# A two-layer streaming encoder on one core: the modulation's first pieces land in spare slots, and three projections of layer 0 run as float32r passes

## The chip, the core and the metric

The kernel runs on one core of a Trainium2 chip. What counts is the device time of one execution in microseconds (us). The kernel before took 2290.78 us, the median of three runs (2288.68 to 2294.38). One more execution was taken with the profiler on; it took 2285.5 us, and all durations below come from it.

## The reference, cut to what matters

x has 256 positions of 2048 channels, c is one row of 2048. Each of two layers computes six modulation rows from c, then an input projection of the normalised and modulated x, whose columns feed four groups of mixers, an output projection, and a gated feed-forward block. The part that matters here is the start of layer 0:

```
c_act = silu(c)
mod = (c_act @ w_mod[l] + b_mod[l]).reshape(bn, 6, d)      # 2048 x 12288
shift_m, scale_m, gate_m = mod[:, 0], mod[:, 1], mod[:, 2]
h = layer_norm(x) * (1.0 + scale_m) + shift_m
proj = h @ w_in[l]                                         # 2048 x 4288
uv, q_c, kv_c, k_r, sb, sc, sh, ag = split(proj)
y_a = gmlp(uv)          # U (512 columns) and V (512)
y_b = attention(q_c, kv_c, k_r)                            # B
y_c = sb * conv3(sc * sh)                                  # E (sb) and C (sc, sh)
y_d = silu(layer_norm(conv31(a * sigmoid(g))))             # D: a, g = split(ag), 1024 columns
```

## The kernel before, in words

All engines work from lists of instructions in a fixed order: a scheduling layer records the program, gives each operation its place on its engine, and adds the waits. TensorE multiplies; VectorE, ScalarE and GpSimd work element by element; SyncE (SP) issues nearly all loads, in order. A load that has to wait for a buffer holds up all loads behind it. Loads take one of eight semaphores in turn, so a load also waits until the one eight places before it has landed.

A product in full float32 ("exact") has one instruction in the program and two matmul records in the trace. The other way is float32r: a float32 weight is cast to float32r (`whi`, ScalarE, L455), the rest is what VectorE subtracts (`wlo`, L456), the activations are split likewise (`hT`, L474 and L475), and three float32r products (hi by hi, hi by lo, lo by hi) take the place of the exact one. `weights` (L420) does one or the other: it loads into a buffer of the `raw` kind (4 of 1 MB) and splits into `whi` and `wlo` tiles (4 of each, 0.5 MB), or, for exact products, loads straight into `whi` and `wlo` tiles without a split.

The modulation runs on VectorE: each step (`mod_step`, L230 to L236) multiplies a loaded tile of w_mod by one value of c_act per partition and adds it to an accumulator (`qacc` or `macc`). TensorE then sums the accumulator's partitions with a column of ones (`ps_mod`), and VectorE adds the bias (L190, L192).

Layer 0 can't wait for the whole modulation. `by_pieces` (L1174) therefore cuts the 2048 channels into pieces of k tiles of 128: two tiles, two, four, four and four (here pieces 0 to 4). `mod_piece` (L238) makes shift and scale of one piece: 16 row tiles of w_mod, four steps to a raw buffer in the small pieces (512 wide) and two in the others (1024 wide), so that the small pieces take 16 steps of 512 and the others 16 of 1024. `finish` in `piece` (L1378) takes the sums, modulates the normalised x (`hF`, half on ScalarE, half on VectorE) and splits it into `hT`.

For each piece TensorE adds the k tiles' share to four projections: D (1024 columns), which keeps four of the six PSUM accumulators through all pieces, and U, V and E (512 each), which use the other two in turn. `side` (L1202) computes their share and adds it to sums in SBUF: ScalarE copies PSUM out (`part`, L1220), VectorE adds (L1221); in the last piece VectorE adds from PSUM (L1217). D's products run in float32r from the fifth k tile on (pieces 2 to 4); U, V and E stay exact in all pieces. The work of a piece is woven in four turns: a quarter of D, then U, V or E after each of the first three; the steps for the next piece's modulation are put between them by shares (`some_mods`), and the next piece's `finish` stands ahead of the fourth quarter of D.

After the last piece: `mix_d` (GLU: two sigmoids on ScalarE, two products on VectorE, then a list of 124 conv taps and the norm as background work), `mix_u`, `gelu_v` and `mix_v` (the gMLP), then the exact projections B (768 columns) and C (1024), during which the background list is worked off at seven and eight entries a unit, and a stream of further modulation rows (w_mod, 1 MB a step) is fed at a rate for each phase (RATES). Then comes the output projection (`out_proj`), whose first 1024 columns are float32r.

Slots are 11 tiles of 0.5 MB for activations. Four of them hold `hF` from the start of layer 0 to the end of C; the other seven stand empty while the pieces run.

Of the kernel before, what the change touches and what calls it, by code (L numbers as in the profile page):

```python
# [13 lines left out]
P = 128  # L14
D = 2048
# [3 lines left out]
KT = D // P  # L19
# [25 lines left out]
PIECES = ((0, 2), (2, 2), (4, 4), (8, 4), (12, 4))  # L45

PLAIN_KT = 4


@with_exitstack  # L50
def encoder_kernel(ctx: ExitStack, tc: tile.TileContext, A: dict, consts: bass.AP, out: bass.AP):
# [14 lines left out]
    def raw_tile(name):  # L66
        return rawp.tile([P, 2048], F32, tag="raw", name=name)
# [7 lines left out]
    def acc_tile(name):  # L75
        return accp.tile([P, 512], F32, tag="acc", name=name)

    def mm(o, lhsT, rhs, start, stop):
        pe.matmul(o, lhsT, rhs, start=start, stop=stop, skip_group_check=True)  # L79
# [4 lines left out]
    def slot(name, dtype=F32):  # L84
        return slotp.tile([P, 1024], dtype, tag="slot", name=name)
# [113 lines left out]
    def sum_cols(l, m, k0, acc):  # L199

        n = acc.shape[1] // P
        ps = ms_tile("ps_mod")
        for j in range(n):
            mm(ps[:, j : j + 1], acc[:, j * P : (j + 1) * P], ones[:, 0:1], True, True)
        mod_cols(l, m, k0, ps, n)
# [24 lines left out]
    def mod_step(acc, w, kt, first):  # L230
        col = cact[:, kt : kt + 1]
        if first:
            i = dve.tensor_scalar(out=acc, in0=w, scalar1=col, scalar2=None, op0=ALU.mult)
        else:
            i = dve.scalar_tensor_tensor(out=acc, in0=w, scalar=col, in1=acc, op0=ALU.mult, op1=ALU.add)  # L235
        held(i, "mod")  # L236

    def mod_piece(l, ms, k0, nkt):  # L238


        n, width = len(ms), nkt * P
        nk = 2048 // (n * width)
        acc = tmpp.tile([P, D], F32, tag="macc", name="qacc", bufs=2)[:, : n * width]
        units = []

        def unit(u):
            raw = raw_tile("wmod").rearrange("p (k m c) -> p k m c", k=nk, m=n)
            for i, m in enumerate(ms):
                c0 = m * D + k0 * P
                nc.sync.dma_start(  # L250
                    out=raw[:, :, i, :],
                    in_=A["w_mod"][l, u * nk * P : (u + 1) * nk * P, c0 : c0 + width].rearrange(
                        "(k p) c -> p k c", p=P
                    ),
                )
            for k in range(nk):
                mod_step(acc, raw[:, k, :, :].rearrange("p m c -> p (m c)"), u * nk + k, u == 0 and k == 0)

        for u in range(KT // nk):
            units.append(lambda u=u: unit(u))  # L260

        def sums():
            for i, m in enumerate(ms):
                sum_cols(l, m, k0, acc[:, i * width : (i + 1) * width])

        return units, sums
# [122 lines left out]
    background = []  # L389
# [21 lines left out]
    def held(i, kind):  # L411

        name, n = hold[kind]
        if n > 0:
            hold[kind][1] = n - 1
            tc.add_manual_dep(i.ins, name, order_dep, reason="the norm is what the next products wait for")
# [45 lines left out]
    def act_pair(name):  # L462

        both = actp.tile([P, 4 * S], F32R, tag="act", name=name).rearrange("p (k h t) -> p k h t", k=2, h=2)
        return [both[:, :, 0, :], both[:, :, 1, :], both]
# [708 lines left out]
    def by_pieces(l, w_in, hF, between, mix_d, mix_u, gelu_v, mix_v, mix_b, mix_c, mix_e):  # L1174


        hf = lambda kt: hF[kt // 4][:, kt % 4, :]
        accD = [acc_tile(f"D{l}_c{i}") for i in range(4)]
        sums = {}
        for g in "UVE":  # L1180
            both = actp.tile([P, 1024], F32, tag="act", name=f"sum{g}")
            sums[g] = [both[:, i * 512 : (i + 1) * 512] for i in range(2)]
        cols = {"U": C_UV, "V": C_UV + 512, "E": C_SB}

        hT[:] = [None] * (PLAIN_KT // 2) + [act_pair("hT") for _ in range((KT - PLAIN_KT) // 2)]

        def terms(kt, part):

            hi, lo = part
            if lo is None:  # L1190
                return [(hi, hf(kt))]
            xh, xl = (h[:, kt % 2, :] for h in hT[kt // 2][:2])
            return [(hi, xh), (hi, xl), (lo, xh)]

        def chan_major(ps, kt, part, blocks, first, last):
            ts = terms(kt, part)
            for i in blocks:
                o = ps[i // 2][:, (i % 2) * S : (i % 2 + 1) * S]
                for n, (w, x) in enumerate(ts):
                    mm(o, w[:, i * P : (i + 1) * P], x, first and n == 0 and i % 2 == 0, last and n == len(ts) - 1)  # L1200

        def side(g, parts, k0, nkt):  # L1202
            ps = [acc_tile(f"{g}{l}_{i}") for i in range(2)]
            for kt, part in parts:
                st, sp = kt == k0, kt == k0 + nkt - 1
                if g == "V":
                    ts = terms(kt, part)
                    for t in range(2):
                        for n, (w, x) in enumerate(ts):
                            mm(ps[t], x[:, t * P : (t + 1) * P], w, st and n == 0, sp and n == len(ts) - 1)  # L1210
                else:
                    chan_major(ps, kt, part, range(4), st, sp)
            for i in range(2):
                if k0 == 0:
                    act.copy(sums[g][i], ps[i])
                elif k0 + nkt == KT:
                    dve.tensor_tensor(out=sums[g][i], in0=ps[i], in1=sums[g][i], op=ALU.add)  # L1217
                else:
                    part = tmp_tile("part")
                    act.copy(part, ps[i])  # L1220
                    dve.tensor_tensor(out=sums[g][i], in0=part, in1=sums[g][i], op=ALU.add)  # L1221

        first = between(0)[1]
        first()
        for q, (k0, nkt) in enumerate(PIECES):
            ahead = between(q + 1) if q + 1 < len(PIECES) else ([], None)
            exact = k0 < PLAIN_KT
            loaded = {}

            def load(g, kt):  # L1230

                c0, width = (C_AG, 1024) if g == "D" else (cols[g], 512)
                nk = min(2048 // width, nkt)
                for j, p in enumerate(weights(w_in, kt, nk, c0, width, exact or g != "D")):
                    loaded[(g, kt + j)] = p

            mods_left = list(ahead[0])
            units = len(mods_left)

            def some_mods(share):  # L1240
                while mods_left and (units - len(mods_left)) < units * share:
                    mods_left.pop(0)()

            def d_part(kt, half):
                if ("D", kt) not in loaded:
                    load("D", kt)
                chan_major(accD, kt, loaded[("D", kt)], range(4 * half, 4 * half + 4), kt == 0, kt == KT - 1)

            turns_d = [(kt, h) for kt in range(k0, k0 + nkt) for h in range(2)]
            n = len(turns_d) // 4  # L1250
            for s in range(4):
                mine = turns_d[s * n : (s + 1) * n]
                if ("D", mine[0][0]) not in loaded:
                    load("D", mine[0][0])
                some_mods((0.3, 0.7, 1.0, 1.0)[s])
                if s == 3 and ahead[1] is not None:
                    ahead[1]()
                for kt, h in mine:
                    d_part(kt, h)
                if s < 3:  # L1260
                    g = "UVE"[s]
                    load(g, k0)
                    some_mods((0.5, 0.85, 1.0)[s])
                    side(g, [(kt, loaded[(g, kt)]) for kt in range(k0, k0 + nkt)], k0, nkt)
        mix_d(accD, None)
        mix_u(sums["U"], None)
        for t in range(2):
            gelu_v(t, sums["V"][t])
        mix_v()
        phase(l, "B")  # L1270
        run(group(w_in, C_Q, 768, f"B{l}", mix_b, hF=hf, bg=STEPS[l]["B"]))
        phase(l, "C")

        def mix_ce(cps, tps):
            mix_c(cps, tps)
            mix_e(sums["E"], None)

        run(group(w_in, C_SC, 1024, f"C{l}", mix_ce, hF=hf, bg=STEPS[l]["C"]))
        drain_background()
# [88 lines left out]
    def piece(q, hF):  # L1368
# [9 lines left out]
        def finish():  # L1378
# [3 lines left out]
            for kt in range(k0, k0 + nkt):  # L1382
# [4 lines left out]
                else:  # L1387
                    dve.tensor_scalar(out=h, in0=h, scalar1=sc, scalar2=sh, op0=ALU.mult, op1=ALU.add)
            for kt in range(max(k0, PLAIN_KT), k0 + nkt, 2):
                split(hT[kt // 2], hF[kt // 4][:, kt % 4 : kt % 4 + 2, :])  # L1390
# [144 lines left out]
```

## Time and profile before

| | |
|---|---|
| time, median of 3 runs | 2290.78 us |
| the profiled execution | 2285.5 us, of it the span 2283.7 us |
| TensorE busy | 2226.7 us (98%) |
| VectorE busy | 1788.8 us (78%) |
| ScalarE busy | 1049.8 us (46%) |
| loaded | 601.16 MB, 264 GB/s over the span |

The page shows busy time by engine and by slice of the span. A view by stage gives, for any stretch of the span, what each engine was busy in it, the granted TensorE clock as a share of full speed, the share of time the 16 DMA engines were busy, and GB/s. A view in order of time lists instructions, merged where the same one repeats (x7): start, time from first start to last end, engine, line, operation, out<-in, shapes, count, and in brackets the idle time before it with what ended it. The start-to-start distance between rows is what an instruction costs its engine; the time of a single one can be some tens of ns longer, as its end overlaps the next. PE is TensorE, PEld its weight loads, DVE VectorE, ACT ScalarE, POOL GpSimd, SPq the loads as SP issues them.

### The profile page before, as it was taken

Reading aid. Unit: us, or ns where it says so; the run is one execution under the profiler, and the core shown is the slowest. Engines: PE = TensorE matmul, PEld = TensorE weight load, DVE = VectorE, ACT = ScalarE, POOL = GpSimd, SP = SyncE. Lnnn points to the kernel's source line nnn. Section 1 sums busy time; section 2 is a strip of 40 time slices with the busy share of each in tenths; the row PEclk is TensorE's granted clock in tenths of the full one; section 3 lists DMA queues with packets and bytes.
Section 4 is the critical chain, followed back from the end, with each engine's and each line's share of the span. In section 5 each row is a group of like instructions: output and inputs, shape, how many; then the busy total and the mean of one; then the engine's idle time right before and its main releaser. Section 6 shows DMA issues by size and latency. Waiting matters only on the chain. (4 is left out here: it accounts for less than half of the span.)

```text
span 2283.7 us, 30024 instructions
## 1 busy us (share of the span) xinstructions
PE 2226.7 (98%) x11682; PEld 1859.8 (81%) x11682; DVE 1788.8 (78%) x2270; ACT 1049.8 (46%) x1525; POOL 35.3 (2%) x59
## 2 busy tenths in 40 slices
PE   5899999999999999999999999999999999999998
PEld 4688886478888888887887999877888888888886
DVE  6878998598888898998976799787776565665676
ACT  2221141355554544544556434556555554454553
POOL 2000000000000000000000000000000000000000
PEclk9999999999999999999999999999999999999999
DMA  9999889778998988888974666876765556555554
GB/s 348 368 335 342 304 301 393 301 267 304 319 329 302 323 312 327 317 316 304 319 258 148 200 214 240 291 268 223 247 223 190 184 182 199 186 196 190 193 194 147
DMA packets 224566, 605.21 MB, mean 265 GB/s; under 512 B 14548, under 2 KB 27076, under 8 KB 202660
## 3 DMA queue, kind: packets, MB, share of 16 engines
q1 hardware_dynamic: 223576, 602.30, 74.7%
q8 instruction: 91, 1.49, 0.3%
q0 software_dynamic: 848, 1.01, 0.1%
q14 instruction: 51, 0.42, 0.0%
HBM read 601.16 MB, written 2.10 MB: 264 GB/s over the span
## 5 line engine op out<-in xcount | busy, mean ns | idle before, releaser
L456 DVE TENSOR_TENSOR wlo<-wraw,whi 128x1024 fp32r<-128x1024 f32 (+1 forms) x624 | 749.6, 1214 | 315.5 <-ACT whi L455 309.4
L455 ACT CAST whi<-wraw 128x1024 fp32r<-128x1024 f32 (+1 forms) x624 | 649.2, 1047 | 727.2 <-PE g_c L79 204.4
L79 PE MATMUL v_c<-hT,whi 128*128 128x512 f32 x1408 | 493.1, 394 | 0.0
L79 PE MATMUL g_c<-hT,whi 128*128 128x512 f32 x1280 | 448.2, 394 | 0.0
L79 PE MATMUL v_c<-hT,wlo 128*128 128x256 f32 x1408 | 394.3, 280 | 0.0
L79 PE MATMUL d<-whi,a 128*128 128x512 f32 x1344 | 387.9, 390 | 0.0
L235 DVE SCALAR_TENSOR_TENSOR macc<-wmod,cact,macc 128x2048 f32<-128x2048 f32 x150 | 351.6, 2344 | 17.1 <-DMA wmod<-in_w_mod_dram 16.8
L79 PE MATMUL g_c<-hT,wlo 128*128 128x256 f32 x1280 | 358.4, 280 | 0.0
L79 PEld LDWEIGHTS v_c<-hT,whi 128*128 128x128 f32 x1408 | 263.9, 187 | 61.0
L79 PEld LDWEIGHTS d<-whi,a 128*128 128x128 f32 x1344 | 252.9, 188 | 52.4
L79 PEld LDWEIGHTS g_c<-hT,whi 128*128 128x128 f32 x1280 | 239.9, 187 | 55.6
L79 PEld LDWEIGHTS v_c<-hT,wlo 128*128 128x128 f32 x1408 | 265.8, 189 | 0.2
L79 PEld LDWEIGHTS g_c<-hT,wlo 128*128 128x128 f32 x1280 | 241.7, 189 | 0.2
L79 PE MATMUL d<-wlo,a 128*128 128x512 f32 x672 | 233.8, 390 | 1.9 <-DVE wlo L456 1.9
L79 PEld LDWEIGHTS d<-wlo,a 128*128 128x128 f32 x672 | 126.6, 188 | 29.1 <-DVE wlo L456 2.7
L79 PE MATMUL o<-whi,a 128*128 128x512 f32 x352 | 102.3, 398 | 2.3 <-ACT whi L455 2.3
L834 DVE SCALAR_TENSOR_TENSOR convD<-gluD,pm,convD 128x237 f32<-128x237 f32 (+26 forms) x240 | 99.0, 458 | 0.5
L474 ACT CAST a<-g 128x512 fp32r<-128x512 f32 x132 | 81.1, 616 | 36.7 <-PE d L79 34.2
L79 PE MATMUL D_c<-hT,whi 128*128 128x256 f32 x448 | 85.7, 292 | 4.0 <-ACT hT L474 3.0
L475 DVE TENSOR_TENSOR a<-g,a 128x512 fp32r<-128x512 f32 x132 | 87.5, 683 | 1.8 <-ACT a L474 1.8
L566 PE MATMUL first<-wexact,hN 128*128 128x512 f32 x192 | 85.7, 596 | 1.5 <-ACT hN L82 1.2
L235 DVE SCALAR_TENSOR_TENSOR qacc<-wmod,cact,qacc 128x1024 f32<-128x1024 f32 (+1 forms) x75 | 80.2, 1070 | 2.4 <-DMA wmod<-in_w_mod_dram 0.4
(311 smaller groups left out, 2462.3 us busy)
## 6 DMA issues: line engine op xcount, KB each, us to landing
wraw<-in_ffn_w_up_dram SPq DMA_DIRECT2D x168, 1024.0 KB, 5.2
wmod<-in_w_mod_dram SPq DMA_DIRECT2D x160, 1024.0 KB, 6.6
wraw<-in_ffn_w_down_dram SPq DMA_DIRECT2D x88, 1024.0 KB, 5.3
wmod<-in_w_mod_dram SPq DMA_DIRECT2D x64, 512.0 KB, 7.9
wraw<-in_w_in_dram SPq DMA_DIRECT2D x30, 1024.0 KB, 5.5
wexact<-in_w_in_dram SPq DMA_DIRECT2D x52, 512.0 KB, 6.7
wraw<-in_w_out_dram SPq DMA_DIRECT2D x24, 1024.0 KB, 7.3
wexact<-in_w_out_dram SPq DMA_DIRECT2D x16, 512.0 KB, 11.0
```

Of the source, the lines that this page charges most:

```text
L79: pe.matmul(o, lhsT, rhs, start=start, stop=stop, skip_group_check=True)
L235: i = dve.scalar_tensor_tensor(out=acc, in0=w, scalar=col, in1=acc, op0=ALU.mult, op1=ALU.add)
L455: held(act.copy(hi[:, :m], r), "cast")
L456: i = dve.tensor_tensor(out=lo[:, :m], in0=r, in1=hi[:, :m].bitcast(F32), op=ALU.subtract)
L474: act.copy(hi, src)
L475: dve.tensor_tensor(out=lo, in0=src, in1=hi.bitcast(F32), op=ALU.subtract)
L566: i = pe.matmul(ps, hN[kt // 4][:, kt % 4, t * P : (t + 1) * P], parts[kt], start=kt == 0, stop=kt == KT - 1, skip_group_check=True,)
L834: dve.scalar_tensor_tensor(out=yd[:, j, 30 - k :], in0=glu[:, j, : S - 30 + k], scalar=CW(k, j), in1=yd[:, j, 30 - k :], op0=ALU.mult, op1 ...
```

## The change

Three edits. First, the modulation pieces from the second on load into slots, half a unit at a time: twice as many loads of half the size, none of which takes a raw buffer. Second, U, V and E of layer 0 are split and run in float32r from the fifth k tile on, as D is; their weights then come through raw buffers, in 1 MB loads. Third, the last piece runs all of D first, then loads U and puts the GLU group (`mix_d`) ahead of U's products, then U, V and E one after the other, with 8 entries of the background list (conv taps) recorded after each of the three.

```diff
+TAPS_ASIDE = 8
...
-        def unit(u):
-            raw = raw_tile("wmod").rearrange("p (k m c) -> p k m c", k=nk, m=n)
+        def land(raw, kt, nk):
+
+            raw = raw.rearrange("p (k m c) -> p k m c", k=nk, m=n)
             for i, m in enumerate(ms):
                 c0 = m * D + k0 * P
                 nc.sync.dma_start(
                     out=raw[:, :, i, :],
...
+                    in_=A["w_mod"][l, kt * P : (kt + nk) * P, c0 : c0 + width].rearrange("(k p) c -> p k c", p=P),
                 )
             for k in range(nk):
-                mod_step(acc, raw[:, k, :, :].rearrange("p m c -> p (m c)"), u * nk + k, u == 0 and k == 0)
+                mod_step(acc, raw[:, k, :, :].rearrange("p m c -> p (m c)"), kt + k, kt + k == 0)
+
+        def unit(u):
+            if k0 == 0:
+                land(raw_tile("wmod"), u * nk, nk)
+                return
+
+            for h in range(2):
+                land(slot("wmod"), u * nk + h * nk // 2, nk // 2)
...
-                for j, p in enumerate(weights(w_in, kt, nk, c0, width, exact or g != "D")):
+                for j, p in enumerate(weights(w_in, kt, nk, c0, width, exact)):
...
             turns_d = [(kt, h) for kt in range(k0, k0 + nkt) for h in range(2)]
+            if k0 + nkt == KT:
+
+                for kt, h in turns_d:
+                    d_part(kt, h)
+                for g in "UVE":
+                    load(g, k0)
+                    if g == "U":
+                        mix_d(accD, None)
+                    side(g, [(kt, loaded[(g, kt)]) for kt in range(k0, k0 + nkt)], k0, nkt)
+                    for _ in range(TAPS_ASIDE):
+                        background.pop(0)()
+                continue
...
-        mix_d(accD, None)
         mix_u(sums["U"], None)
```

In the changed program, as it is built, the order on the engines differs in the pieces as follows. On TensorE in piece 1 seven of the eight column sums for piece 2 stand ahead of E and the eighth behind it; in pieces 2 and 3 the order is half of D, U, V, nearly all of D's other half, the column sums, the rest of D, E. On VectorE in pieces 2 and 3, counted from the last `hT`, it is: a step, a subtraction (D), five steps, two subtractions (U), four steps, U's two sums with a step behind each, two subtractions (V), two steps, two subtractions (D), V's two sums, two steps, and at the turn to the next piece E's two subtractions and the first of the next D between the modulation columns and `hT`.

## What was predicted

> **What bounds the kernel now.** I read the page first, then the busy time by stage, then TensorE and VectorE in order of time.
>
> ```profile
> span 2283.7 us, 30024 instructions
> ...
> PE 2226.7 (98%) x11682; PEld 1859.8 (81%) x11682; DVE 1788.8 (78%) x2270; ACT 1049.8 (46%) x1525; POOL 35.3 (2%) x59
> ```
>
> TensorE (PE) is the bound nearly everywhere: 57 us idle in the whole span. The stages that the change touches, cut where the pieces of the input projection begin (52, 84.5, 123.4, 158.2) and where B starts (189.5):
>
> ```profile
> core 0: us, PE busy (x) PEld busy (x) DVE busy (x) ACT busy (x) POOL busy (x), PEclk, DMA share, GB/s
> ...
> 51.70:84.50 32.80, 25.06 (x105) 18.47 (x105) 28.83 (x38) 8.36 (x14) 5.74 (x11) 0.89 1.01 364
> 84.50:123.40 38.90, 36.60 (x197) 30.18 (x196) 32.71 (x36) 9.49 (x14) 0.00 (x0) 0.96 1.02 372
> 123.40:158.20 34.80, 34.46 (x190) 28.31 (x190) 28.62 (x31) 9.42 (x14) 0.00 (x0) 1.00 0.93 332
> 158.20:189.50 31.30, 31.30 (x173) 25.91 (x172) 16.00 (x13) 3.89 (x4) 0.00 (x0) 1.00 0.96 338
> 189.50:325.40 135.90, 135.78 (x655) 115.58 (x653) 127.88 (x223) 32.26 (x63) 6.52 (x7) 1.00 0.88 318
> 325.40:380.60 55.20, 52.09 (x227) 41.31 (x225) 49.71 (x45) 18.59 (x25) 0.00 (x0) 0.94 0.91 340
> ```
>
> Rows one to four are pieces 1 to 4 (piece 0 comes before). In piece 1 VectorE (DVE) is the busiest engine with 28.83 of 32.8 us; in pieces 2 and 3 TensorE (36.60 of 38.9, 34.46 of 34.8), VectorE (32.71, 28.62) and the DMA (share 1.02, 0.93) lie close together; piece 4 is TensorE alone. So a saving on TensorE in pieces 2 and 3 is worth only the distance to the next of these three, and what the change loads onto VectorE has 4 to 6 us of room a piece.
>
> **What the float32r passes save on TensorE.**
>
> ```profile
> 126.22 7.07 PE L79 MATMUL U<-hF,wexact 128*128 128x256 f32 x32
> ...
> 135.16 7.03 PE L79 MATMUL V<-wexact,hF 128*128 128x512 f32 x16
> ...
> 146.25 7.07 PE L79 MATMUL E<-hF,wexact 128*128 128x256 f32 x32
> ...
> 153.16 1.84 PE L79 MATMUL ps_mod<-ones,qacc 128*128 128x1 f32 x16
> ...
> 187.34 0.40 PE L79 MATMUL D_c<-hT,whi 128*128 128x256 f32 x2
> ...
> 187.58 0.28 PE L79 MATMUL D_c<-hT,wlo 128*128 128x256 f32 x1
> ...
> 187.70 0.40 PE L79 MATMUL D_c<-hT,whi 128*128 128x256 f32 x2
> ```
>
> A piece of four k tiles has 16 exact products for U, each two records: 7.07 us. As three float32r passes each, the D rows show the rate: 187.34 to 187.70, three products in 0.36 us, 0.12 each. U becomes 48 x 0.12 = 5.76 us, E the same. V streams 512 columns; the rate for that stands in the output projection:
>
> ```profile
> 327.86 1.07 PE L79 MATMUL o<-whi,a 128*128 128x512 f32 x4
> 328.77 0.62 PE L79 MATMUL o<-wlo,a 128*128 128x512 f32 x2
> 329.22 1.07 PE L79 MATMUL o<-whi,a 128*128 128x512 f32 x4
> ```
>
> Six in 1.36 us, 0.227 each: V becomes 24 x 0.227 = 5.45 us. Saved: 1.3 + 1.6 + 1.3 = 4.2 us a piece, 12.6 us for pieces 2 to 4. TensorE's work in a piece, with D (96 x 0.12 = 11.5) and the modulation sums (1.84), falls to 30.3 us.
>
> **What it adds on VectorE.** Each of U, V and E now brings two casts (ScalarE, which is busy 9.4 us of a piece and has room) and two subtractions (VectorE): six more of each a piece.
>
> ```profile
> 76.20 0.69 DVE L1221 TENSOR_TENSOR sumV<-part,sumV 128x512 f32<-128x512 f32 x1
> 76.81 1.28 DVE L235 SCALAR_TENSOR_TENSOR qacc<-wmod,cact,qacc 128x1024 f32<-128x1024 f32 x1
> 78.01 0.68 DVE L1221 TENSOR_TENSOR sumE<-part,sumE 128x512 f32<-128x512 f32 x1
> ...
> 83.26 1.28 DVE L475 TENSOR_TENSOR hT<-hF,hT 128x512 fp32r<-128x512 f32 x2
> 84.46 1.22 DVE L456 TENSOR_TENSOR wlo<-wraw,whi 128x1024 fp32r<-128x1024 f32 x1
> 85.60 9.20 DVE L235 SCALAR_TENSOR_TENSOR qacc<-wmod,cact,qacc 128x1024 f32<-128x1024 f32 x7
> ```
>
> From start to start a subtraction takes 1.14 us (84.46 to 85.60), a modulation step 1.31 in a run (9.20/7) and 1.20 ahead of another operation, a sum 0.61. Pieces 2 and 3 averaged (32.71 + 28.62)/2 = 30.7 us of VectorE; with 6 x 1.14 it is 37.5 us. That is more than TensorE's 30.3 and more than the DMA needs: a piece loads 16 modulation steps of 0.52 MB and 5.2 MB of weights, 13.6 MB, 37 us at the 372 GB/s of piece 2's row. **VectorE becomes the bound of pieces 2 and 3.** Its order is fixed by the built program, and it has to stand once a piece: after the last step TensorE sums the columns (half of the 1.84 us, with the hand-over some 1.2 us) before the first modulation column can be made. 38.7 us.
>
> **The clock.** In the changed program VectorE's order after hT is: a step, a subtraction, five steps, U's two subtractions, four steps, U's sums with a step behind each, V's two subtractions, and so on. By the durations above (the first step of a piece, without accumulation, 0.7) U's second subtraction ends 10.5 us after hT and V's first 20.4 us after it, while U is done by 13.5 to 15: TensorE stands for 5 to 7 us in each of pieces 2 and 3. What such a pause does shows in piece 1:
>
> ```profile
> 66.99 5.32 PE L79 MATMUL V<-wexact,hF 128*128 128x512 f32 x8 [2.58 <-DMA wexact<-in_w_in_dram]
> 74.33 3.69 PE L79 MATMUL E<-hF,wexact 128*128 128x256 f32 x16 [2.01 <-DMA wexact<-in_w_in_dram]
> 78.14 1.95 PE L79 MATMUL ps_mod<-ones,qacc 128*128 128x1 f32 x16
> 83.12 1.46 PE L79 MATMUL D_c<-hT,whi 128*128 128x256 f32 x4 [3.03 <-ACT hT L474]
> ```
>
> ```profile
> 66.00:67.00 1.00, 0.01 (x1) 0.04 (x1) 1.00 (x3) 0.00 (x0) 0.00 (x0) 0.96 1.06 412
> 67.00:68.00 1.00, 1.00 (x2) 0.48 (x3) 0.96 (x2) 0.00 (x0) 0.00 (x0) 0.50 1.05 403
> ...
> 70.00:71.00 1.00, 1.00 (x3) 0.35 (x3) 0.96 (x2) 0.00 (x0) 0.00 (x0) 0.84 0.95 356
> ```
>
> After 2.58 us of idling the granted clock was 0.50 from 67 until into the 70:71 slice (0.84, so two thirds of it at full speed), some 3.3 us. At half rate for that long V, started 20.4 us after hT, ends at 27.5 instead of 25.9; ScalarE's copy of it is there 0.8 later; VectorE, which comes to V's sums 26.4 us after hT, then waits 1.8 us. A piece is 40.5 us so, 38.7 if the clock stays up. The Trainium skill, TensorE: Matmul & The Clock Gate (What's actually happening), says the array falls to half rate after an idle window of about 3.4 us and needs as long of work to come back; the trace agrees with the length, and shows the fall after 2.58 us already. By that page both pauses would be cold, 40.5 us a piece; if the windows happened to miss them, the sum below would be 3.6 us less.
>
> **Piece by piece, against the profiled execution (2285.5 us, span 2283.7).**
>
> Piece 0 and the empty slots: **0**. The modulation pieces now land in seven slots of 0.5 MB instead of sharing four buffers of 1 MB with the weights: 3.5 MB ahead instead of up to 4, but the weights no longer wait for them. That helps only where VectorE waited for a load. It did not in piece 1; its longest wait there was for a product of TensorE:
>
> ```profile
> 64.20 0.69 DVE L1221 TENSOR_TENSOR sumU<-part,sumU 128x512 f32<-128x512 f32 x1 [1.08 <-ACT part L1220]
> ```
>
> ```profile
> 101.70 0.88 SPq L250 DMA_DIRECT2D wmod<-in_w_mod_dram  x2
> ```
>
> SP issues 56 more loads, at 0.44 us or less each, 25 us over the 110 us of pieces 0 to 3; it hides in SP's own waits:
>
> ```profile
> SPq L250 <- DVE qacc L235: 46.7, 20, 7.8
> ```
>
> Piece 1, **+3 us**: in the changed program seven of the eight column sums stand on TensorE ahead of E, the eighth behind it; before, E (74.33 to 78.0) filled the time in which VectorE finished its steps. Now TensorE waits from V's end (72.3) for the last step (about 77.1), then does the sums (1.7) and E (3.6), and only the last sum lets the scale column go: at 82.7 instead of 80.1, from a pause of 5 us, so up to 1.5 later if cold. The hT that ended at 84.5 ends at about 87.5. Bounds: +1 if E slips in warm, +5 if all of it is cold.
>
> Pieces 2 and 3, **2 x 40.5 - 73.7 = +7 us** (73.7 = 38.9 + 34.8). Bounds: 2 x 37.5, no wait at all, +1.3; 42 each, +10.
>
> Piece 4, **-1.5 us**: no modulation to add, so TensorE sets it: 11.5 + 5.76 + 5.45 + 5.76 = 28.5 us, and it starts some 1.3 us after hT, behind E of piece 3, which waited for its subtractions at the turn: 29.8 instead of 31.3. The GLU group first puts sigmoid, gate and 24 of its 124 conv taps beside U, V and E, where VectorE had 15 us free (16.00 of 31.3). V's and E's splits stand behind the gate on ScalarE and VectorE: ready some 16 and 19 us after D began, needed at 17 and 23. Bounds: -2.8 and +2.
>
> B and C, **+0.5 us**: taken from VectorE are 24 taps:
>
> ```profile
> L834 DVE SCALAR_TENSOR_TENSOR convD<-gluD,pm,convD 128x237 f32<-128x237 f32 (+26 forms) x240 | 99.0, 458 | 0.5
> ```
>
> 11 us at 458 ns, but TensorE is busy there 135.78 of 135.9, so it hides them already. The gMLP products stand after 11 products of B now instead of 23, 5 us in, and the gate's norm behind E's sums reaches them about then: 0 to 3.
>
> Output projection, 0: its 192 products and the modulation sums (3.6) need 192 x 0.227 + 3.6 = 47.2 us and took 55.2. If a lighter VectorE in C opened this, 8 us would come back; but its steps and splits (49.71 of 55.2 busy) are unchanged and stand behind C's end as before. Bounds -8 and +2.
>
> Sum: 3 + 7 - 1.5 + 0.5 = **+9 us**. I take off half a microsecond for the wait for U's sum in piece 1, part of which may go: +8.5. The profiled execution would give 2294; its 2285.5 lies 5.3 under the median of 2290.78, and on the median I get **2299 us**.
>
> **Rivals.**
>
> *The front breaks even.* VectorE's own waits in pieces 1 to 3 vanish because the loads lie further ahead, the clock stays up. For it: the rows of pieces 1 to 3 show 4.0 + 6.2 + 6.2 us of VectorE idle. Against: most of it came from sums waiting for TensorE, not from loads. All lower bounds but the output projection's: 1 + 1.3 - 2.8 = -0.5, up to +4: 2290 to 2295.
>
> *TensorE's saving comes through, faster.* It decides if VectorE runs without a gap from piece 1 on, so that hT of piece 4 comes by 155.5 (51.7 plus 103.8 of work: 30.7 x 2 + 28.8 + 13.6 of subtractions until then) instead of 158.2. Then the pieces end 4 us earlier, and a projection that is reached with VectorE less behind gives back up to 8: -4 to -12, 2279 to 2287.
>
> *Small loads.* They took long to land:
>
> ```profile
> wmod<-in_w_mod_dram SPq DMA_DIRECT2D x64, 512.0 KB, 7.9
> ```
>
> If 256 KB still took 7.9 us, eight under way would move 8 x 0.262 MB / 7.9 us = 265 GB/s, and 13.6 MB would take 51 us: +20 in pieces 2 and 3, 2310 and more. Against it: the queue was full (share 1.02), so those 7.9 us were mostly waiting in line, and less in line lands sooner.
>
> **How the numbers follow.** Forecast 0.48 (2295 to 2304), break-even 0.28, saving comes through 0.14, small loads or more cold stretches 0.10. A measurement of this kernel tells about 0.3%, 6.9 us, from no change. Faster by more than that: most of the third case, 0.11. Slower by more: three quarters of the forecast and the last, 0.46. Within: 0.43. The range leaves out half of the two outer cases: 2284 to 2307.
>
> **What would show it.** Right: in pieces 2 and 3 VectorE busy over 37 us of about 40, TensorE idle before V with the cause wlo, granted clock near 0.5 behind it; in piece 1 TensorE waiting for qacc ahead of E; B starting near 198. Wrong: B starting at 189 or sooner; VectorE waiting for wmod in pieces 2 and 3 (then it is the loads); a projection much shorter than 55 us.

## The result, and the profile after

The changed kernel takes 2299.36 us (median of 9 runs, 2292.66 to 2302.73), beside 2288.68 us for the kernel before in the same series. The ratio is 1.0046 [1.0034, 1.0059]: 10.5 us slower, with an interval of 8 to 13.5. The prediction was a shift of +8.5 us. Its 2299.0 is this close to 2299.36 only because it stood on a median of before that was 2.1 us higher; the shift itself is 2 us short. The profiled execution took 2300.09 us.

The page of the changed kernel, its span and busy times, and its row for the small loads of w_mod (count, KB each, median us from issue to landing):

```profile
span 2298.0 us, 30400 instructions
...
PE 2224.3 (97%) x11802; PEld 1869.8 (81%) x11802; DVE 1807.0 (79%) x2288; ACT 1067.1 (46%) x1543; POOL 35.6 (2%) x59
...
wmod<-in_w_mod_dram SPq DMA_DIRECT2D x112, 256.0 KB, 6.2
```

TensorE is busy 2.4 us less than before and the span is 14.3 us longer, so the time went into waiting. The view by stage shows where. Its rows are pieces 1 to 4, cut where hT ends, then B and C, then the float32r part of the output projection:

```profile
core 0: us, PE busy (x) PEld busy (x) DVE busy (x) ACT busy (x) POOL busy (x), PEclk, DMA share, GB/s
52.20:89.60 37.40, 27.83 (x102) 20.92 (x103) 28.11 (x35) 7.94 (x14) 5.99 (x11) 0.84 0.96 344
89.60:129.80 40.20, 33.73 (x220) 31.42 (x220) 36.16 (x38) 14.23 (x18) 0.00 (x0) 0.86 0.94 340
129.80:170.00 40.20, 32.82 (x229) 30.45 (x228) 36.04 (x38) 15.39 (x20) 0.00 (x0) 0.92 0.81 287
170.00:200.10 30.10, 30.10 (x232) 29.14 (x231) 24.45 (x33) 17.35 (x23) 0.00 (x0) 1.00 0.75 252
200.10:337.80 137.70, 135.54 (x654) 115.58 (x652) 128.75 (x213) 28.24 (x56) 6.53 (x7) 1.00 0.87 319
337.80:394.50 56.70, 52.35 (x226) 41.32 (x225) 50.05 (x45) 15.89 (x20) 0.00 (x0) 0.94 0.94 359
```

In pieces 2 and 3 VectorE is now the busiest engine (36 of 40.2 us), TensorE stands for 6.5 and 7.4 us, and the granted clock averages 0.86 and 0.92. Piece 4 is full TensorE work. Against before, stage by stage: piece 1 **+5.15** (VectorE goes on behind hT at 89.61, before at 84.46), pieces 2 and 3 together **+6.7** (80.4, were 73.7), piece 4 **-1.3**, B and C **+1.9**, the projection **+1.4**, all the rest of the program +0.4. The sum is 14.3. These are two single executions; the medians are 10.5 us apart, so some 4 us of the 14.3 belong to these two executions and not to the change.

The prediction named what the rows should show. Piece 1 on TensorE, in order of time:

```profile
66.58 5.37 PE L81 MATMUL V<-wexact,hF 128*128 128x512 f32 x8 [2.09 <-DMA wexact<-in_w_in_dram]
76.81 2.73 PE L81 MATMUL ps_mod<-ones,qacc 128*128 128x1 f32 x14 [4.86 <-DVE qacc L237]
79.39 6.03 PE L81 MATMUL E<-hF,wexact 128*128 128x256 f32 x16
85.27 0.28 PE L81 MATMUL ps_mod<-ones,qacc 128*128 128x1 f32 x2
```

TensorE waits 4.86 us for the last modulation step ahead of seven column sums, and E behind them takes 6.03 us where it took 3.69. Piece 3 on VectorE and then on TensorE:

```profile
154.33 2.35 DVE L465 TENSOR_TENSOR wlo<-wraw,whi 128x1024 fp32r<-128x1024 f32 x2
158.41 1.37 DVE L1230 TENSOR_TENSOR sumV<-part,sumV 128x512 f32<-128x512 f32 x2 [1.72 <-ACT part L1229]
159.69 2.60 DVE L237 SCALAR_TENSOR_TENSOR qacc<-wmod,cact,qacc 128x1024 f32<-128x1024 f32 x2
164.41 0.16 DVE L192 TENSOR_TENSOR mod<-ps_mod,bcol 128x4 f32<-128x4 f32 x1 [2.12 <-PE ps_mod L81]
164.49 2.36 DVE L465 TENSOR_TENSOR wlo<-wraw,whi 128x1024 fp32r<-128x1024 f32 x2
```

```profile
139.79 0.39 PE L81 MATMUL U<-hT,wlo 128*128 128x256 f32 x1 [2.62 <-DVE wlo L465]
...
147.13 0.73 PE L81 MATMUL V<-whi,hT 128*128 128x512 f32 x2 [1.81 <-ACT whi L464]
150.82 0.80 PE L81 MATMUL V<-wlo,hT 128*128 128x512 f32 x1 [2.95 <-DVE wlo L465]
...
158.04 0.39 PE L81 MATMUL V<-wlo,hT 128*128 128x512 f32 x1
```

VectorE has two pauses in the whole piece, 1.72 us for the copy of V and 2.12 us for the column sums; between them it is never idle. TensorE waits for the subtractions (wlo) of U and V, and V's 22 passes from 150.82 on take 7.6 us, where 22 x 0.227 would be 5.0. So the waits are those that were named. Two figures are not: VectorE is busy 36 us a piece and not over 37, and B starts at 200.5 and not near 198.

### The profile page after: what moved, and what is told of

Read it like the earlier page. It is cut to its first block, busy times and chain, and to the rows that moved or that the text cites. A ratio compares the mean times of both kernels' runs of the same rounds, so it can differ in the third digit from the quotient of the medians.

```text
span 2298.0 us, 30400 instructions
## 1 busy us (share of the span) xinstructions
PE 2224.3 (97%) x11802; PEld 1869.8 (81%) x11802; DVE 1807.0 (79%) x2288; ACT 1067.1 (46%) x1543; POOL 35.6 (2%) x59
## 5 line engine op out<-in xcount | busy, mean ns | idle before, releaser
L465 DVE TENSOR_TENSOR wlo<-wraw,whi 128x1024 fp32r<-128x1024 f32 (+1 forms) x642 | 770.6, 1214 | 308.1 <-ACT whi L464 302.2
L464 ACT CAST whi<-wraw 128x1024 fp32r<-128x1024 f32 (+1 forms) x642 | 666.9, 1047 | 709.1 <-PE g_c L81 195.6
L843 DVE SCALAR_TENSOR_TENSOR convD<-gluD,pm,convD 128x251 f32<-128x251 f32 (+25 forms) x240 | 100.5, 460 | 0.4
L483 ACT CAST a<-g 128x512 fp32r<-128x512 f32 x132 | 81.1, 616 | 34.7 <-PE d L81 32.0
L81 PEld LDWEIGHTS o<-whi,a 128*128 128x128 f32 x352 | 67.2, 192 | 18.2 <-ACT whi L464 4.1
```

Source lines behind the costliest of these rows:

```text
L464: held(act.copy(hi[:, :m], r), "cast")
L465: i = dve.tensor_tensor(out=lo[:, :m], in0=r, in1=hi[:, :m].bitcast(F32), op=ALU.subtract)
L483: act.copy(hi, src)
L843: dve.scalar_tensor_tensor(out=yd[:, j, 30 - k :], in0=glu[:, j, : S - 30 + k], scalar=CW(k, j), in1=yd[:, j, 30 - k :], op0=ALU.mult, op1 ...
```

## The experiments

All stages of all kernels, from the rows of their traces. Piece 1 is given by the start of VectorE's hT subtraction, pieces 2 and 3 from one such start to the next, piece 4 from there to B's first product, "B, C" to the projection's first product, the projection up to its first exact product. The long rest of the program is the same in all of them and took between 1898.5 and 1906.4 us from one profiled execution to the next. So stages are read from the traces and totals from the ratios.

| kernel | piece 1 at | 2 | 3 | 4 | B, C | projection | ratio to before |
|---|---|---|---|---|---|---|---|
| before | 83.3 | 38.9 | 34.7 | 33.1 | 135.4 | 55.2 | 1 |
| changed | 88.4 | 40.2 | 40.1 | 31.8 | 137.3 | 56.7 | 1.0046 [1.0034, 1.0059] |
| e1_slots_only | 88.6 | 38.5 | 36.2 | 33.1 | 135.8 | 55.9 | 1.0014 [1.0004, 1.0025] |
| e2_passes_only | 83.8 | 38.9 | 40.6 | 31.8 | 135.1 | 56.9 | 1.0018 [1.0006, 1.0029] |
| e3_order_only | 85.7 | 38.8 | 37.9 | 33.0 | 135.6 | 55.4 | 1.0005 [0.9993, 1.0018] |
| e4_last_piece | 83.5 | 39.4 | 37.9 | 29.3 | 135.4 | 58.4 | 1.0014 [1.0003, 1.0025] |
| f1_no_subtractions | 87.6 | 34.5 | 38.0 | 33.4 | 137.2 | 56.8 | 1.0026 [1.0016, 1.0036] |
| f2_e_ahead | 82.1 | 39.7 | 40.2 | 31.8 | 136.5 | 56.0 | 1.0023 [1.0008, 1.0037] |
| f3_warm | 88.8 | 42.1 | 42.6 | 31.5 | 136.1 | 55.8 | 1.0045 [1.0032, 1.0058] |
| f4_last_held | 83.9 | 39.5 | 37.8 | 30.4 | 134.9 | 58.4 | 1.0010 [1.0000, 1.0021] |
| g1_last_held_both | 83.2 | 38.9 | 34.7 | 29.4 | 136.7 | 57.5 | 0.9993 [0.9980, 1.0006] |
| g2_last_woven | 83.7 | 39.4 | 34.7 | 29.4 | 135.1 | 54.9 | 0.9987 [0.9975, 0.9999] |
| h1_no_third | 88.3 | 40.3 | 40.1 | 31.8 | 135.4 | 56.1 | 1.0033 [1.0020, 1.0045] |
| h2_best | 82.5 | 38.3 | 34.3 | 29.4 | 135.1 | 54.9 | 0.9966 [0.9955, 0.9978] |

**The three edits, one by one.** The theory is that of the prediction (A): VectorE bounds pieces 2 and 3, and piece 1 loses by TensorE's order. The rivals were the transfers, and the work behind the pieces.

e1: `land` and `unit` of the change on the kernel before, nothing else.

> The kernel before with the first edit alone: modulation pieces land in slots, U, V and E stay exact, the last piece stays woven. Theory A (the order of piece 1): this edit alone puts seven of the eight column sums ahead of E in piece 1, so the hT that ended at 84.5 ends at 88 to 90; pieces 2 and 3 keep TensorE as the bound and take the 73.7 us of before, give or take 3; total +2 to +7. Theory B (the loss of piece 1 comes from the transfers): the queue of VectorE would show waits for wmod, and pieces 2 and 3 would lose as much again, total +10 or more. Rival C (the slots help): VectorE stands less in pieces 2 and 3, they fall to 70 or less, total 0 or below.

e2: one line on the kernel before.

```diff
-                for j, p in enumerate(weights(w_in, kt, nk, c0, width, exact or g != "D")):
+                for j, p in enumerate(weights(w_in, kt, nk, c0, width, exact)):
```

> The kernel before with the second edit alone: U, V and E in float32r passes from the fifth k tile on, modulation pieces still in raw buffers, the last piece still woven. Theory A (VectorE's subtractions bound pieces 2 and 3): piece 1 ends as before, hT at 84 to 85; pieces 2 and 3 take 40 to 42 us each with 36 us of VectorE, +7 to +10; piece 4 falls by 1 to 3; total +5 to +8. Theory B (the passes are free and all loss is in the slots): pieces 2 and 3 take 73.7 or less, total -4 to 0. Rival C (the raw buffers, now shared by steps and weights, hold up the loads): pieces 2 and 3 take 45 or more each, waits for wmod or wraw, total +12 or more.

e3: the block `if k0 + nkt == KT` of the change and the moved `mix_d`, on the kernel before.

> The kernel before with the third edit alone: in the last piece all of D first, the GLU group ahead of U, 24 conv taps recorded between U, V and E; U, V and E exact, no slots. Theory A: nothing on TensorE's path changes, pieces end where they did (189.5, give or take 1), B and C and the output projection keep 135.9 and 55.2; total -1 to +1. Theory C (the 3.4 us that the changed kernel lost behind the pieces comes from this edit): B and C 2 us longer, the output projection 1.5 longer, with waits for dgB and p; total +2 to +5.

Measured: the slots alone make the whole loss of piece 1 (88.6) and 1.5 us in piece 3. The passes alone leave piece 1 as it was (83.8) and make the loss of pieces 2 and 3: 79.5 us, were 73.6. That it all falls in piece 3 (40.6) and none in piece 2 (38.9) was not expected. The sum, too, lies a little under the 80 to 84 us expected, and the total, +4 us by the ratio, under the +5 to +8; the total of e1, +3, is in its range. So the prediction's +3 for piece 1 and +7 for pieces 2 and 3 belong to two different edits. The rival of the transfers falls for pieces 2 and 3: their loss comes in e2, which has no small loads, and hardly in e1, which has them. In e2 ScalarE's casts wait for loads, up to 7.5 us at a time, but VectorE doesn't: its longest pause in the two pieces, 2.1 us, is for the column sums.

The third edit alone can't be told from no change by its ratio, but its trace showed two losses that theory A did not have, and B starts at 195.3, not at 189.5. Piece 3 took 37.9 us; what that is shows in the fourth group. And piece 1 ended 2.4 us late, though this edit changes nothing there. E stood behind a pause of 2.13 us and ran at half clock, where in the kernel before, behind 2.01 us, it took 3.69 us:

```profile
75.43 5.38 PE L81 MATMUL E<-hF,wexact 128*128 128x256 f32 x16 [2.13 <-DMA wexact<-in_w_in_dram]
```

Some 1.7 of the 2.4 us are that. Where such a pause lies in the clock's windows is chance, as the last section shows, so one trace of piece 1 can be off by this much.

**Piece 1: is it the order?** f2 puts E back ahead of the column sums and leaves all else of the changed kernel (in `sum_cols`; i is a column sum of piece 2's modulation, last_e holds E's last product of piece 1).

```diff
+            if last_e and (l, k0) == (0, 4):
+                tc.add_manual_dep(i.ins, last_e[-1], order_dep, reason="E of the piece before comes first")
```

> The changed kernel with one thing put back: in piece 1 the eight column sums stand behind E on TensorE, as before the change. Theory A (seven sums ahead of E make TensorE wait and then run E at half clock): E runs while VectorE finishes its steps, hT ends at 84 to 86 instead of 89.6, and all that follows moves up by 4 to 5 us; total 3 to 5 us below the changed kernel. Rival B (VectorE's steps or their loads are late with slots): hT still ends at 88 or later, total as the changed kernel.

TensorE in piece 1 of this kernel:

```profile
66.88 5.37 PE L81 MATMUL V<-wexact,hF 128*128 128x512 f32 x8 [2.36 <-DMA wexact<-in_w_in_dram]
73.56 3.69 PE L81 MATMUL E<-hF,wexact 128*128 128x256 f32 x16 [1.31 <-DMA wexact<-in_w_in_dram]
77.08 1.84 PE L81 MATMUL ps_mod<-ones,qacc 128*128 128x1 f32 x16
```

E starts 5.8 us earlier and takes 3.69 us, the sums follow without a pause, and piece 1 ends at 82.1, 6.3 us earlier than in the changed kernel and 1.2 earlier than before. The ratio falls from 1.0046 to 1.0023, 5 us (the two intervals overlap only from 1.0034 to 1.0037). Slots as such cost piece 1 nothing; the order into which they led the scheduling layer does.

**Pieces 2 and 3: is it VectorE?** f1 leaves out the subtractions of U, V and E and nothing else of their passes (`lo = hi`).

> The changed kernel without the subtractions of U, V and E in pieces 2 to 4: their lo part is left out and the cast weight is used in its place, so TensorE runs the same three passes and VectorE has six operations less a piece (the sums of U, V and E are not the reference's). Theory A (VectorE's subtractions bound pieces 2 and 3): VectorE's 36.1 us a piece fall to about 29, and pieces 2 and 3 from 40.2 to 34 to 37 us each, until TensorE or the loads (13.6 MB a piece) are next; total 6 to 12 us below the changed kernel. Rival B (the casts on ScalarE, the buffers or the slower clock bound them): they stay at 39 or more, total within 3 us of the changed kernel.

By stage, pieces 2 and 3 of f1, and its only wait of TensorE in piece 3:

```profile
88.90:123.40 34.50, 28.88 (x200) 27.04 (x200) 28.06 (x31) 13.01 (x17) 0.00 (x0) 0.90 0.94 342
123.40:161.40 38.00, 32.55 (x234) 30.86 (x234) 30.53 (x33) 15.59 (x21) 0.00 (x0) 0.91 0.99 363
```

```profile
143.71 7.75 PE L81 MATMUL V<-whi,hT 128*128 128x512 f32 x24 [5.45 <-ACT whi L464]
```

Piece 2 falls by 5.7 us to 34.5, as theory A had it. Piece 3 falls only by 2.1 to 38.0, a little over the range of A and under that of B: with VectorE out of the way, V's cast weights are late (5.45 us): their casts waited 3.73 us for the load, at a DMA share of 0.99. VectorE is the bound of both pieces; in piece 3 the loads stand 2 us behind it. In all 4.6 us by the ratios, less than the 6 to 12 expected, and piece 4 gives 1.6 us of it back.

f3 fills the place in which TensorE waits for V's splits with six products, `mm(warm, ident, cst[:, 512:1024], True, True)`, between U and V.

> The changed kernel with six products more between U and V in pieces 2 and 3, each 128x512 exact of two constant tiles into a tile that nobody reads, some 5.3 us of TensorE in the place where it waited 4.8 us for V's splits. VectorE's work is the same; two subtractions move behind the scale column. Theory A (V at half clock costs 1.8 us a piece, as the prediction has it): the granted clock stays at 1.0 through V, V takes 5.5 us from its first lo product instead of 8, VectorE waits less for V's sums, pieces 2 and 3 take 38.2 to 39.2 each; total 2 to 4 us below the changed kernel. Rival B (VectorE's work alone sets the piece): pieces within 0.5 us of 40.2 though the clock is up, total the same or above.

TensorE in piece 3 of f3, the filling, V's first and V's last row:

```profile
150.15 5.31 PE L81 MATMUL warm<-cst 128*128 128x512 f32 x12
154.89 1.49 PE L81 MATMUL V<-whi,hT 128*128 128x512 f32 x4
...
160.53 0.39 PE L81 MATMUL V<-wlo,hT 128*128 128x512 f32 x1
```

V's 24 passes now run through in 6.0 us (154.89 to 160.92), 5.45 at the full rate; in the changed kernel 22 of them took 7.6. So the pause before V costs V 2.6 us, 1 us more than the prediction's 1.6. The gain did not come: the pieces took 42 us. The filling moved VectorE's order (V's first sum now stands ahead of E's subtractions, U's subtractions later behind hT), VectorE waits 2.18 us for V's copy all the same, and U starts later. So f3 doesn't show what a warm V is worth with the order unchanged; that stays open.

**The last piece: where do 4 us of TensorE go?** e4 is e3 with the passes in piece 4 alone: `exact or (g != "D" and k0 + nkt < KT)`.

> The kernel before with the third edit and the passes of U, V and E in the last piece alone, where VectorE has no modulation steps; pieces 2 and 3 exact, no slots. Theory A: TensorE's saving of 4.2 us comes through here as far as splits are in time: piece 4 falls from 31.3 to 28 to 30 us, B starts at 186 to 188; total -1 to -4. Theory C (what is behind the pieces eats it): the pieces end earlier but B, C or the output projection grow by as much, total 0 or above.

Piece 4 falls to 29.3 us, but piece 3 is at 37.9 as in e3, and B starts where it did. Two subtractions of D's weights (the third and fourth k tile) had come ahead of hT on VectorE. f4 orders the last piece's subtractions behind it, load by load, with the kernel's own `held` (the next two come after a named instruction, here the subtraction of hT):

```diff
+                if k0 + nkt == KT and (g, kt) != ("D", k0):
+                    hold["split"] = [last_split[0], 2]
```

> The kernel before with the third edit and the passes in the last piece alone, and the last piece's splits from the second load on ordered behind hT: in the run that only lacked this, two of D's subtractions stood between the modulation columns and hT, and piece 3 took 37.85 us instead of 34.7. Theory A (these two are what ate the gain): piece 3 is back at 34.5 to 35.5, piece 4 stays at 29 to 30.5, B starts at 186 to 187.5 (at 190 with the splits ahead), total -1 to -4 against the kernel before. Rival B (the splits are only shifted, D then waits for them): piece 4 grows to 32 or more, B starts at 189 to 191, total 0 or above.

Theory A was wrong in this form: piece 3 stays at 37.8, and B starts at 191.7. ScalarE and VectorE of f4, in order of time, show why:

```profile
155.09 1.05 ACT L457 CAST whi<-wraw 128x1024 fp32r<-128x1024 f32 x1
158.66 1.04 ACT L457 CAST whi<-wraw 128x1024 fp32r<-128x1024 f32 x1 [2.53 <-PE D_c L81]
159.61 1.09 ACT L84 ACTIVATE hF<-hF,mod,mod 128x256 f32<-128x256 f32 x2
```

```profile
156.48 0.74 DVE L1405 TENSOR_SCALAR hF<-hF,mod,mod 128x256 f32<-128x256 f32 x2
161.24 1.29 DVE L479 TENSOR_TENSOR hT<-hF,hT 128x512 fp32r<-128x512 f32 x2 [4.02 <-ACT hT L478]
```

The modulation columns are there at 156.4. But on ScalarE a cast of D's weight stands ahead of hF; it waits 2.53 us for TensorE to free its buffer, hF starts at 159.61, and VectorE waits 4.02 us for hT. In e3 and e4 the same cast waits 2.53 us in this place. So the casts have to be held; holding the subtractions alone leaves piece 3 where it was. g1 holds both (`hold["cast"]` as well); g2 does so without the third edit, that is, with the old weave.

> As the run before it (the kernel before with the third edit and the passes in the last piece alone), but with ScalarE's casts ordered behind hT as well as VectorE's subtractions, from the last piece's second load on. In the run before, one cast of D's weight stood ahead of hF and hT on ScalarE and waited 2.53 us for its buffer, and hT 4.02 us for it. Theory A (this cast is what ate the gain): piece 3 is back at 34.5 to 35.5 us, piece 4 takes 29 to 31, B starts at 186 to 188, total -1 to -4 against the kernel before. Rival B (piece 4 then waits for the later casts): piece 4 at 32.5 or more, B at 189 or later, total -1 or above. If both stages shrink and the total doesn't, the output projection has taken it: 58.4 us there in the two runs of this kind, 55.2 before.

> The kernel before with the passes of U, V and E in the last piece alone, woven as before (no third edit), the last piece's casts and subtractions from the second load on ordered behind hT. Theory A: piece 3 at 34.5 to 35.5, piece 4 at 31 to 32 (31.8 in the run with all passes and the weave), against 33.1 before; B starts at 188 to 189, total 0 to -2. Rival B (the third edit is what makes the passes pay in the last piece or not): the same within 1 us of the kernel with the third edit and both holds. If the output projection stays at 55 to 56 here and is 58 there, the third edit lengthens it.

Both bring piece 3 back to 34.7 and piece 4 to 29.4, and B starts at 186.2 and 187.2 (189.9 before). So 3 to 4 us of TensorE's 4.2 do come through in the last piece, with either order. Theory A and its price for the cast are right (3.1 us from f4 to g1); the expectation that the weave would keep piece 4 at 31 was wrong. g1 then loses them again: B and C 136.7, the projection 57.5, together 3.5 us more than before, and its ratio can't be told from 1. g2 keeps them.

**The three edits without the third.** h1 is e1 and e2 together.

> The changed kernel without its third edit: slots and passes in pieces 2 to 4, the last piece woven as before. Theory A (the three edits cost in their own places): piece 1 ends at 88 to 90 as with slots alone, pieces 2 and 3 take 40 to 41 each, piece 4 31 to 32; from B's start to the exact products of the output projection 191 to 192 us, as in the runs with passes and without the third edit, against 194.0 in the changed kernel; total 1 to 3 us below the changed kernel. Rival B (the 3 us behind the pieces do not hang on the third edit): 193 to 195 there, total as the changed kernel within 1 us.

From B's start to the exact projection it takes 191.4 us against 194.0 in the changed kernel, as expected. In the totals this hardly shows: 2299.0 us, ratio 1.0033, and the intervals overlap. Of the kernels with both the third edit and passes, five (changed, e4, f1, f4, g1) take 193.4 to 194.2 us there and two (f2, f3) 192.6 and 191.9; those that lack one of the two take 190.0 to 192.0. So there is a loss of some 2 us with the third edit, but it is not the same for all. Part of it can be read from the waits of TensorE in the changed kernel (us in total, times, longest):

```profile
PE o L81 <- ACT whi L464: 3.3, 2, 2.5
...
PE ps_pT L1110 <- DVE p L1101: 1.1, 1, 1.1
PE ps_rkv L81 <- DVE dgB L1006: 1.1, 1, 1.1
```

The first is in the projection, where the kernel before waits 2.3 us for casts. The other two are in B and C; neither the kernel before nor h1 nor any other kernel without the third edit has them. VectorE's work has moved to these stages: of the modulation steps for later rows (2.35 us each) the kernel before does 5 in piece 4, 23 in B and C and 12 in the projection, the changed kernel 2, 25 and 13. Of the conv taps it has done only 10 before B starts, since nine subtractions now stand beside them in piece 4. h1 has 24 steps in B and C and 13 in the projection without the two waits, so the steps alone don't explain them; why VectorE comes late to these two places is not settled.

**A version that beats both.** h2 is g2 with the slots, and with E ahead of the sums as in f2.

> The woven last piece with passes and both holds, and on top of it the slots with E put ahead of the column sums in piece 1. Theory A (slots cost only by that order, and help once it is put right): piece 1 ends at 82 to 83 instead of 83.7, pieces 2 and 3 at 38.5 and 34.7 to 36.2, B starts at 186 to 188; total between 1 us below and 1 us above the same kernel without slots, 2 to 5 below the kernel before. Rival B (slots cost in piece 3 as well, 36.2 instead of 34.7 with slots alone): B starts at 188 or later, total as the kernel before.

Its pieces 1 to 4 by stage:

```profile
52.20:83.80 31.60, 24.32 (x101) 18.01 (x100) 28.77 (x37) 8.13 (x13) 5.98 (x11) 0.91 1.02 367
83.80:122.10 38.30, 36.86 (x197) 30.84 (x196) 32.68 (x35) 9.50 (x14) 0.00 (x0) 0.94 1.05 387
122.10:156.40 34.30, 34.14 (x194) 28.36 (x193) 28.68 (x30) 10.26 (x15) 0.00 (x0) 1.00 1.02 379
156.40:184.00 27.60, 27.60 (x211) 26.64 (x210) 20.89 (x18) 9.12 (x10) 0.00 (x0) 1.00 0.76 262
```

B starts at 184.5, 5.4 us earlier than before and 16 earlier than in the changed kernel. The ratio is 0.9966 [0.9955, 0.9978]: 2282.25 us, some 8 us below before, more than the 2 to 5 expected. Against g2, which lacks only the slots and their order, B starts 2.7 us earlier, where at most 1 us was expected: the slots do help, a little in each of pieces 1 to 3. TensorE is the bound of pieces 3 and 4 again, and VectorE has 5.6 and 6.7 us of room there.

## Why the prediction was right

- **VectorE becomes the bound of pieces 2 and 3: shown.** 7 us were predicted and 6.7 measured; without the subtractions 5.7 and 2.1 us are gone (f1). Within the sum of 40.5 a piece the terms were: VectorE's work 37.5 (36.1 inside the cuts), the stand at the column sums 1.2 (2.12), the cold V 1.8 (a pause of 1.72). The column sums cost 0.9 more than the term, the work 1.4 less; that the total came out so close is in part these errors cancelling.
- **The clock:** V's pause brought it to 0.50 as said, and V lost 2.6 us, for which 1.6 were taken (5.0 us of it at half instead of 3.3). VectorE's pause of 1.72 us fits the 1.8 of the prediction, but by luck: V lost 1 us more, and the copy, put 0.8 us behind V's end, began ahead of it (157.79, V's end is at 158.4), since it comes in two halves. That a warm V would give the pause back was not shown (f3).
- **Piece 1, +3: the mis-sized term; it measured +5.15.** The order was read rightly, seven sums ahead of E, and f2 shows that it is the whole of it. The pause of 5 us and its cause were right. What was too small is the price of the cold clock, "up to 1.5 later": E took 6.03 us for 3.69 and seven sums 2.6 for 1.6, together 3.3 us more. The bound of +5 stood for this case and was just passed. The edit was also named wrongly: "the empty slots: 0" holds for the loads, but it is the slots that made the order (e1).
- **Piece 4, -1.5: right (-1.3).** The splits were ready in time.
- **B and C +0.5 and the projection 0: together +3.3 in the profile. This step failed.** It took 24 conv taps, 11 us, from VectorE in B and C, left the projection's work as it was, and saw no modulation in piece 4. But the kernel before does five steps for later rows in piece 4, and the changed kernel only two. So B and C have nine taps less (4 us) and two steps more (4.7 us), the projection one step more. VectorE's work in B and C rose from 127.88 to 128.75 us, and TensorE, which stood 0.1 us there, stands 2.2, in the two waits shown under h1. Why it is these two is open.
- **The total.** In the traces the stages add up to +14.3 where the prediction has +9 before it takes off half a microsecond. The medians' +10.5 is nearer to +8.5 than the stages are to their terms, which is luck.
- **Small loads: refuted.** The 256 KB loads landed in 6.2 us instead of 7.9 for 512 KB, and no wait of VectorE in pieces 2 and 3 was for wmod.
- **"TensorE's saving comes through"** failed here for the reason given, VectorE. Where VectorE is free, in piece 4, it comes through: 3.7 us of 4.2 (g1, g2), once no cast stands ahead of hT.

## What to carry to other kernels

A cheaper product on the bound engine is worth only the distance to the next engine, and its preparation (casts and subtractions) is paid on the others: put it where these have room, here the one piece of five that has no modulation of a next piece to add. After an edit, read each engine's order around the places where one piece hands over to the next: a cast that waits for a buffer, or sums that wait for the last step, can cost as much when they stand ahead of the hand-over as the work that was saved (here 3.1 and 5.15 us, against 4.2 a piece). Then fix such a place by an order, and measure the edit again; here the same two ideas, with the passes in the last piece alone, went from 10 us slower to 8 us faster.

## What the runs showed of the hardware

The granted clock falls to half and comes back only at fixed instants, one window of 3.41 us or several apart. The granted clock of the changed kernel in piece 1, after the pause of 4.86 us, and in piece 3, around the end of that of 2.95:

```profile
77.00:78.00 1.00, 1.00 (x8) 1.00 (x7) 0.35 (x1) 0.00 (x0) 0.00 (x0) 0.65 1.05 389
78.00:79.00 1.00, 1.00 (x7) 1.00 (x6) 0.16 (x1) 0.00 (x0) 0.00 (x0) 0.50 1.07 391
...
83.00:84.00 1.00, 1.00 (x4) 0.82 (x3) 0.00 (x0) 0.00 (x0) 0.00 (x0) 0.50 1.05 389
84.00:85.00 1.00, 1.00 (x6) 0.88 (x5) 0.00 (x0) 0.40 (x1) 0.00 (x0) 0.94 1.04 383
```

```profile
150.00:151.00 1.00, 0.18 (x1) 0.18 (x2) 1.00 (x2) 0.00 (x0) 0.00 (x0) 0.50 1.03 385
...
155.50:156.00 0.50, 0.50 (x3) 0.36 (x3) 0.50 (x2) 0.00 (x0) 0.00 (x0) 0.69 1.02 401
```

In piece 1 the clock fell at 77.30, half a microsecond after the sums had begun, and came back at 84.13. In piece 3 it is at half in the whole row from 150 on, though V starts only at 150.82: it had fallen inside the pause, at 148.98 by rows of half a microsecond, and it came back at 155.81. Both stretches are 6.83 us. The stretch of 3.3 us in the kernel before, which the prediction shows, is 3.42 by such rows (66.91 to 70.33). In the first 200 us of the changed kernel, from its piece 1 on, the falls are at 67.06, 77.30, 87.54, 108.02 and 148.98 and the returns at 70.47, 84.13, 94.37, 114.85 and 155.81. Any two of these lie a whole multiple of 3.413 us apart (from 67.06 to 155.81 it is 26 times that), and so they do in each of the other 13 traces.

So where a pause lies counts as well as how long it is. That of 2.01 us ahead of E in the kernel before lay across a boundary of two windows (73.74) and E ran at full clock; that of 2.13 us in e3 lay inside one (72.56 to 75.98), and the clock fell at its end. The window that ended with the fall at 67.06 had 1.3 us of TensorE's work in it, that before the fall in e3 also 1.3. The clock was down for a second window where the first was not full of products of 256 or 512 columns: behind 148.98 V began only 1.8 us into it, and behind 77.30 it held 2.1 us of sums of one column and 1.3 us of E. Whether the sums count for less was not tested by itself.

The Trainium skill, TensorE: Matmul & The Clock Gate (What's actually happening), gives a free-running window of about 3.4 us, one idle window for the fall and one busy window for the return. The traces agree with the window and its length; they differ in the fall, for which a window with 1.3 us of work was idle enough.
